# A hybrid HGRN2 and RWKV-7 layer: the transposes of values and keys, and the 64-token level, moved into the runs of HGRN's level products

## The chip, the core and the metric

The program runs on one core of a Trainium2 chip. The metric is the device time of one execution in microseconds. The core's engines are TensorE (PE in the profile; its weight loads are shown as PEld), VectorE (DVE), ScalarE (ACT), GpSimd (POOL) and SyncE (SP), which here only issues DMAs. They work side by side and wait for each other by semaphores.

## The reference, cut to what matters

The layer takes 2048 tokens of 1024 channels. After a norm and one input projection, half of the channels go through HGRN2, half through RWKV-7; one output projection and a feed-forward part with a convolution follow. HGRN2 is, for each of its 4 heads of 128 channels and in chunks of tokens:

```
f = lb + (1 - lb) * sigmoid(f_raw);  q = silu(q_raw) * 128**-0.5;  k = 1 - f;  v = i_raw;  logf = log(f)

def step(S, inp):                 # one chunk
    qb, kb, vb, gb = inp
    b = jnp.cumsum(gb, axis=2)
    dec = exp(b_t - b_s) for s <= t, else 0
    A = jnp.einsum('bhtk,bhsk,bhtsk->bhts', qb, kb, dec)
    o = jnp.einsum('bhts,bhsv->bhtv', A, vb) + jnp.einsum('bhtk,bhkv->bhtv', qb * jnp.exp(b), S)
    S = jnp.exp(b_last)[..., None] * S + jnp.einsum('bhsk,bhsv->bhkv', kb * jnp.exp(b_last - b), vb)
    return S, o

o = o * rsqrt(mean(o * o) + eps) * norm_w * silu(g_raw)
```

RWKV-7 is a second recurrence, with a matrix inverse of 32 by 32 and 64 by 64 in each chunk; the change does not touch it.

## The kernel before

The first phase (`phase1`) holds the input projection, both recurrences and three quarters of the output projection; it fills about the first half of the span. The second phase holds the rest of the output projection and the feed-forward part; the change doesn't touch it. Three generators run side by side in the first phase: `dense` (projections), `rw_stream` (RWKV, 8 pieces of 512 tokens and 4 heads each) and `hg_stream` (HGRN, 16 units: 4 blocks of 512 tokens by 4 heads). The loop at the end of `phase1` takes in each round one step of RWKV, one step of HGRN (each up to the generator's next `yield`) and then dense work for a credit of TICK = 2000 ns, at 648 ns for each step of three matmuls:

```python
        while any(alive.values()):
            for key, g in (("r", rw_), ("h", hg_)):
                if alive[key]:
                    ...
                        next(g)
            ...
            fill(TICK)
```

So the program text of the loop is nine dense products, a step of RWKV, a step of HGRN, nine dense products and so on. A scheduler then sets each engine's order from this text. A dense product (`mm3`, L270 to L272) is three matmuls of 128 by 128 by 512 that together have the precision of float32; L270, L271 and L272 stand for its three parts. PSUM has two banks of kind "hg" for HGRN, two of kind "pj" for the projection and two double banks of kind "rw".

A unit of HGRN (`hg_unit`) computes the products of a chunk by levels, so that no decay has to be divided by: level l pairs the two halves of each group of 2 x 2^l tokens. `scaled(l)` makes the operand X of a level on VectorE (for level 0 partly on ScalarE, the copies hX and Sf) from q, k and the running products of decays Pf and Sf; `level` are the products of 32 tokens by 32 or 16 columns for levels 0 to 4 (L990), `across` those of level 5 (L997), and the level of 64 tokens (level 6) has 64 by 64 products (L1046). The steps of a unit before the change are these:

- k = 1 - f (L947); values transposed into a bank (L952), copied to VT by ScalarE; then level operands 0, 1, 2, one step each
- a bank with the products of q and k within a token and levels 0 to 2 (L990, 64 products); VectorE takes them into A
- level operands 3, 4, 5, one step each; a second bank with levels 3, 4 (L990, 32 products) and 5 (L997, 8 products); ScalarE copies them and A into Af
- X of level 6, k * Sf and q * Pf on VectorE
- keys transposed into a third bank (L1044), the 64-token products into a fourth (L1046); ScalarE copies KT and the block of Af
- the state products KT by VT (L1055) and the chain of states SH on VectorE (L1057); the output products (L1064 by Af, L1065 by SH); squares, their mean by the matrix unit (L1083, L1084), Ln and Exp on ScalarE, the scaling, and a store of the result (L1078)

The result is built in a buffer that it shares with k (tag "hk"), so the next unit's k waits for the store. PSUM results are copied by `act` (L122). Ln and Exp, Sigmoid and Tanh, and Silu are in different function tables of ScalarE; `act` puts a table load (L118) where the program text goes over to another one. In RWKV's step before the state chain, matmuls L834 read the copies ZT, L847 read TTs; their results are copied as UV and M, which L867 and L881 read. L905 and L910 are the state chain's products, eight pairs one after the other, with VectorE between them.

Of the kernel before, what the change touches and what calls it, by code (L numbers as in the profile page):

```python
# [7 lines left out]
F32 = mybir.dt.float32  # L8
# [3 lines left out]
AF = mybir.ActivationFunctionType  # L12
# [6 lines left out]
P = 128  # L19
# [3 lines left out]
BLK = 512  # L23
# [44 lines left out]
def tile_layer(ctx, tc, consts, x, norm1_w, w_in, hg_lb_logits, hg_norm_w, rw_shift_mu, rw_w0, rw_w2,  # L68
# [4 lines left out]
    V, S, TE = nc.vector, nc.scalar, nc.tensor  # L73
# [200 lines left out]
    def phase1(c1):  # L274
# [22 lines left out]
        def bank(kind):  # L297
            return ps.tile([P, 512], F32, tag=kind, name=kind, bufs=2)
# [645 lines left out]
        def hg_unit(nb, j):  # L944
# [3 lines left out]

            VT = rp.tile([P, 4, P], F32, tag="VT", name="VT")
            tp = bank("hg")  # L950
            for b in range(4):
                TE.transpose(tp[:, b * P:(b + 1) * P], v[:, b * P:(b + 1) * P], ident)  # L952
            act(VT, tp.rearrange("p (b t) -> p b t", t=P), AF.Copy)
            yield
# [4 lines left out]

            def scaled(l):  # L960

                m = 1 << l
                X = rp.tile([P, BLK], F32, tag="hX", name="hX", bufs=3)
# [71 lines left out]
            yield  # L1035
            X = scaled(6)
            V.tensor_mul(k, k, Sf)
            V.tensor_mul(q, q, Pf)
            yield
            KT = rp.tile([P, 4, P], F32, tag="Sf", name="KT")  # L1040
            tp = bank("hg")
            lp = bank("hg")
            for b in range(4):
                TE.transpose(tp[:, b * P:(b + 1) * P], k[:, b * P:(b + 1) * P], ident)  # L1044
            for b in range(4):
                TE.matmul(lp[0:64, b * 64:b * 64 + 64], X[:, b * P:b * P + 64], X[:, b * P + 64:b * P + 128],  # L1046
                          start=True, stop=True, tile_position=(0, 0))
            act(KT, tp.rearrange("p (b t) -> p b t", t=P), AF.Copy)
            act(Af[0:64, :, 64:128], lp[0:64, 0:256].rearrange("p (b t) -> p b t", t=64), AF.Copy)
# [575 lines left out]
```

## Time and profile before

| | us |
|---|---|
| median of 3 runs | 2649.24 (2648.57 to 2652.3) |
| the profiled execution | 2645.42 |
| its span | 2643.6 |
| granted clock of TensorE, mean | 0.994 |
| PE busy | 2547.0 |
| VectorE busy | 1963.7 |
| ScalarE busy | 1372.7 |
| GpSimd busy | 382.1 |

The span is the time from the first to the last instruction of the profiled execution; the device time has 1.82 us around it. Lines of a timeline have the start, the length, the engine, the line of the kernel, the operation, output <- inputs, tile and shape. Lengths of matmuls overlap, since the next one starts while the one before drains.

### The profile page before, as it was taken

To read this page: it belongs to the slowest core of one execution; us is meant where nothing else is said; L and a number is where in the kernel's file an instruction comes from. 1 tells how busy PE (TensorE), PEld (TensorE's weight loads), DVE (VectorE), ACT (ScalarE), POOL (GpSimd) and SP (SyncE) were. 2 spreads that over 40 slices of the span, in tenths; PEclk is the share of its full clock that TensorE was granted. 3 is DMA by queue.
4 is the path that set the end of the run, shared out by engine and by line. 5 is a ranking of instruction groups with operands and counts; after the bars stand their busy time and mean duration, and the time that the engine had idled before them with its cause. 6 is when DMAs were issued, how large, how long until landed. Compare 5 with 4: busy or idle time off the path is not lost.

```text
span 2643.6 us, 51054 instructions
## 1 busy us (share of the span) xinstructions
PE 2547.0 (96%) x19467; PEld 2046.8 (77%) x19467; DVE 1963.7 (74%) x3744; ACT 1372.7 (52%) x2258; POOL 382.1 (14%) x686
## 2 busy tenths in 40 slices
PE   7999999999999999899899999999999999999998
PEld 5877777777777767777678888887888887888887
DVE  4868677676576765777678789988988887766556
ACT  5555444555545555344466654556554544545444
POOL 6433222212222122232100000000000000000000
PEclk9999999999999999999999999999999999999999
DMA  8846463555655565845583467747763553998655
GB/s 304 239 147 195 152 168 116 143 159 205 190 173 138 174 212 179 261 151 150 181 287 124 136 221 257 240 154 232 245 203 129 171 171 128 334 321 283 200 191 187
DMA packets 380298, 518.98 MB, mean 196 GB/s; under 512 B 114463, under 2 KB 211093, under 8 KB 380053
## 3 DMA queue, kind: packets, MB, share of 16 engines
q1 hardware_dynamic: 325521, 337.38, 40.1%
q0 software_dynamic: 54464, 178.32, 20.9%
q8 instruction: 153, 2.51, 0.4%
q14 instruction: 92, 0.75, 0.1%
q10 hardware_dynamic: 68, 0.02, 0.0%
HBM read 372.99 MB, written 134.22 MB: 192 GB/s over the span
## 4 chain that ended last, share of the span: by engine, by line
PE 70%; DVE 11%; ACT 8%; DMA 7%; issue 3%; POOL 0%; SPq 0%; DVEq 0%; ACTq 0%; POOLq 0%
PE pj L270 7%; PE pj L271 7%; PE pj L272 6%; PE ua L270 5%; PE ua L272 5%; PE ua L271 5%; PE da L271 3%; PE da L272 3%; PE da L270 3%; PE ud L271 2%; PE ud L270 2%; PE ud L272 2%; PE db L272 2%; PE db L271 2%; PE db L270 2%
## 5 line engine op out<-in xcount | busy, mean ns | idle before, releaser
L270 PE MATMUL pj<-hh,wh 128*128 128x512 f32 x960 | 391.6, 408 | 6.1 <-ACT rkv L122 4.0
L271 PE MATMUL pj<-hl,wh 128*128 128x512 f32 x960 | 377.4, 393 | 0.0
L272 PE MATMUL pj<-hh,wl 128*128 128x512 f32 x960 | 377.4, 393 | 0.0
L270 PE MATMUL ua<-Bh,uwh 128*128 128x512 f32 x704 | 276.4, 393 | 3.5 <-ACT m L122 2.2
L272 PE MATMUL ua<-Bh,uwl 128*128 128x512 f32 x704 | 274.3, 390 | 0.0
L271 PE MATMUL ua<-Bl,uwh 128*128 128x512 f32 x704 | 274.1, 389 | 0.0
L270 PEld LDWEIGHTS pj<-hh,wh 128*128 128x128 f32 x960 | 180.9, 189 | 54.5 <-issue 7.0
L272 PEld LDWEIGHTS pj<-hh,wl 128*128 128x128 f32 x960 | 180.8, 188 | 39.4 <-DMA wl<-Win171l 0.3
L271 PEld LDWEIGHTS pj<-hl,wh 128*128 128x128 f32 x960 | 181.0, 189 | 35.0 <-DVE hl L488 0.5
L254 ACT CAST uwh<-uraw 128x512 fp32r<-128x512 f32 x220 | 134.3, 617 | 135.0 <-PE ua L271 55.7
L255 DVE TENSOR_TENSOR dal<-draw,dah 128x512 fp32r<-128x512 f32 x138 | 95.2, 690 | 108.3 <-ACT dah L254 105.7
L255 DVE TENSOR_TENSOR uwl<-uraw,uwh 128x512 fp32r<-128x512 f32 x220 | 147.1, 684 | 34.3 <-ACT uwh L254 34.3
L254 ACT CAST dah<-draw 128x512 fp32r<-128x512 f32 x138 | 85.8, 621 | 160.0 <-PE da L271 75.5
L270 PEld LDWEIGHTS ua<-Bh,uwh 128*128 128x128 f32 x704 | 132.2, 188 | 33.9 <-ACT m L122 5.6
L272 PEld LDWEIGHTS ua<-Bh,uwl 128*128 128x128 f32 x704 | 132.2, 188 | 28.1 <-DVE uwl L255 0.4
L271 PEld LDWEIGHTS ua<-Bl,uwh 128*128 128x128 f32 x704 | 132.3, 188 | 26.7
L270 PE MATMUL ud<-Bh,uwh 128*128 128x512 f32 x352 | 138.0, 392 | 0.0
L1495 POOL DMA_DIRECT2D gd<-y x2 | 1.1, 542 | 943.1 <-DVE y L1493 943.1
L272 PE MATMUL ud<-Bh,uwl 128*128 128x512 f32 x352 | 137.1, 390 | 0.0
L271 PE MATMUL ud<-Bl,uwh 128*128 128x512 f32 x352 | 137.0, 389 | 0.0
L271 PE MATMUL da<-dbl,dah 128*128 128x512 f32 x332 | 129.4, 390 | 0.2 <-DVE dbl L255 0.2
L272 PE MATMUL da<-dbh,dal 128*128 128x512 f32 x332 | 129.2, 389 | 0.0
(582 smaller groups left out, 6203.0 us busy)
## 6 DMA issues: line engine op xcount, KB each, us to landing
uraw<-in_w_up_dram SPq DMA_DIRECT2D x176, 256.0 KB, 3.2
woraw<-in_w_out_dram POOLq DMA_DIRECT2D x96, 256.0 KB, 3.6
br<-gd SPq DMA_DIRECT2D x88, 256.0 KB, 4.3
draw<-Sg SPq DMA_DIRECT2D x88, 256.0 KB, 3.0
draw<-Tw SPq DMA_DIRECT2D x88, 256.0 KB, 3.9
gd<-y SPq DMA_DIRECT2D x86, 256.0 KB, 3.0
Sg<-br SPq DMA_DIRECT2D x72, 256.0 KB, 2.2
xt<-x1d SPq DMA_DIRECT2D x32, 512.0 KB, 6.5
```

Of the source, the lines that this page charges most:

```text
L254: S.copy(hi, src)
L255: V.tensor_sub(lo, src, hi.bitcast(F32))
L270: TE.matmul(acc, lh, rh, start=first, stop=False, skip_group_check=skip)
L271: TE.matmul(acc, lh, rl, start=False, stop=False, skip_group_check=skip)
L272: TE.matmul(acc, ll, rh, start=False, stop=last, skip_group_check=skip)
L1495: (dma if end is None else nc.gpsimd.dma_start)(gd_[2 * h + b][fb * P:(fb + 1) * P, :], ys[0][:, b * BLK:(b + 1) * BLK])
```

## The change

Nothing that is computed changes. Three things are moved.

- The transposes of the values leave the start of a unit and stand behind the products of levels 0 to 2, in the same step. A new helper `turned` holds the transposes and the copy, for values and keys alike (L957 in the changed kernel, where L990 has become L992, L997 is L999 and L1046 is L1036).
- Level 6 and the products k * Sf and q * Pf are made before the second bank is filled; the 64-token products go into the second bank's columns 256 to 512, behind levels 3 to 5, and the transposes of the keys follow in the same step. A unit so takes 7 banks of PSUM, not 8, and 13 steps, not 15.
- X of level 6 gets the buffer of SH, since the three buffers of hX are taken by levels 3 to 5.

```diff
-            VT = rp.tile([P, 4, P], F32, tag="VT", name="VT")
-            tp = bank("hg")
-            for b in range(4):
-                TE.transpose(tp[:, b * P:(b + 1) * P], v[:, b * P:(b + 1) * P], ident)
-            act(VT, tp.rearrange("p (b t) -> p b t", t=P), AF.Copy)
-            yield
...
+            def turned(tag, name, src):
+                t_ = rp.tile([P, 4, P], F32, tag=tag, name=name)
+                tp = bank("hg")
+                for b in range(4):
+                    TE.transpose(tp[:, b * P:(b + 1) * P], src[:, b * P:(b + 1) * P], ident)
+                act(t_, tp.rearrange("p (b t) -> p b t", t=P), AF.Copy)
+                return t_
+
             def scaled(l):
...
-                X = rp.tile([P, BLK], F32, tag="hX", name="hX", bufs=3)
+                X = (rp.tile([P, BLK], F32, tag="SH", name="hX6") if l == 6 else
+                     rp.tile([P, BLK], F32, tag="hX", name="hX", bufs=3))
...
             for l in range(3):
                 level(l1, l * 64, Xs[l], Xs[l], l)
+            VT = turned("VT", "VT", v)
             V.tensor_mul(A, ...)
...
             for l in range(3, 6):
                 Xs.append(scaled(l))
                 yield
+            X = scaled(6)
+            V.tensor_mul(k, k, Sf)
+            V.tensor_mul(q, q, Pf)
+            yield
             l1 = bank("hg")
             for l in range(3, 5):
                 level(l1, (l - 3) * 64, Xs[l - 3], Xs[l - 3], l)
             across(l1, 128, Xs[2])
+            for b in range(4):
+                TE.matmul(l1[0:64, 256 + b * 64:320 + b * 64], X[:, b * P:b * P + 64], X[:, b * P + 64:b * P + 128],
+                          start=True, stop=True, tile_position=(0, 0))
+            KT = turned("Sf", "KT", k)
...
-            yield
-            X = scaled(6)
-            V.tensor_mul(k, k, Sf)
-            V.tensor_mul(q, q, Pf)
-            yield
-            KT = rp.tile([P, 4, P], F32, tag="Sf", name="KT")
-            tp = bank("hg")
-            lp = bank("hg")
-            for b in range(4):
-                TE.transpose(...)
-            for b in range(4):
-                TE.matmul(lp[0:64, b * 64:b * 64 + 64], X[...], X[...], ...)
-            act(KT, tp.rearrange("p (b t) -> p b t", t=P), AF.Copy)
-            act(Af[0:64, :, 64:128], lp[0:64, 0:256].rearrange("p (b t) -> p b t", t=64), AF.Copy)
+            act(Af[0:64, :, 64:128], l1[0:64, 256:512].rearrange("p (b t) -> p b t", t=64), AF.Copy)
```

How the order on the engines changes is seen at three places. On PE, the first unit's second bank (L990 and L997) and its keys (L1044) and 64-token products (L1046), with dense products (L270 to L272, outputs pj) around them, before:

```order
374 L271 MATMUL pj<-hl,wh 128x512
375 L272 MATMUL pj<-hh,wl 128x512
376 L990 MATMUL hg<-hX 32x16 x32
377 L997 MATMUL hg<-hX 32x32 x8
378 L270 MATMUL pj<-hh,wh 128x512
...
395 L272 MATMUL pj<-hh,wl 128x512
396 L1044 MATMUL hg<-ident,hk 128x128 x4
397 L1046 MATMUL hg<-hX 64x64 x4
398 L270 MATMUL pj<-hh,wh 128x512
```

and the same place of the changed kernel:

```order
374 L271 MATMUL pj<-hl,wh 128x512
375 L272 MATMUL pj<-hh,wl 128x512
376 L992 MATMUL hg<-hX 32x16 x32
377 L999 MATMUL hg<-hX 32x32 x8
378 L1036 MATMUL hg<-hX_1399 64x64 x4
379 L957 MATMUL hg<-ident,hk 128x128 x4
380 L270 MATMUL pj<-hh,wh 128x512
```

The keys' transposes and the 64-token products have come forward by 18 dense products, into one run with the second bank, the narrow ones first. On PE, the values' transposes of the same unit stood alone before, between dense products:

```order
294 L271 MATMUL pj<-hl,wh 128x512
295 L272 MATMUL pj<-hh,wl 128x512
296 L952 MATMUL hg<-ident,hv 128x128 x4
297 L270 MATMUL pj<-hh,wh 128x512
298 L271 MATMUL pj<-hl,wh 128x512
```

and now stand behind the first bank's 64 products:

```order
323 L271 MATMUL pj<-hl,wh 128x512
324 L272 MATMUL pj<-hh,wl 128x512
325 L992 MATMUL hg<-hq,hk 32x32 x16
326 L992 MATMUL hg<-hX 32x16 x48
327 L957 MATMUL hg<-ident,hv 128x128 x4
328 L270 MATMUL pj<-hh,wh 128x512
```

Over the whole phase there are 247 runs of RWKV's and HGRN's products between dense products before and 213 after. On ScalarE, the first RWKV piece's copies TTs, UV and M, with HGRN's copy hX among them, before:

```order
104 L122 ACTIVATE TTs<-rw 32x8x32 x4
105 L122 ACTIVATE rkv_1763<-pj,omu 128x512
106 L254 CAST wh<-wraw 128x512
107 L122 ACTIVATE hX<-hk 128x256
108 L122 ACTIVATE UV<-rw 64x4x128 x4
109 L122 ACTIVATE M<-rw 128x8x64
```

and after:

```order
104 L122 ACTIVATE TTs<-rw 32x8x32 x2
105 L122 ACTIVATE hX<-hk 128x256
106 L122 ACTIVATE TTs<-rw 32x8x32 x2
107 L254 CAST wh<-wraw 128x512
108 L122 ACTIVATE rkv_1778<-pj,omu 128x512
109 L118 ACT_TABLE_LOAD
110 L122 ACTIVATE UV<-rw 64x4x128 x4
111 L122 ACTIVATE M<-rw 128x8x64
```

The copy hX has come ahead of two of the copies of TTs, and a table load stands ahead of UV: HGRN's steps meet other steps of RWKV than before. The table loads of the whole program are 53 before and 63 after. The loop has 383 rounds in both; HGRN ends in round 383 before and in round 379 after.

More of the change, by code (lines that the diff above doesn't have):

```diff
@@ L1034, in hg_unit @@
                 act(Af[c0:c0 + 32, :, c0:c0 + 32], A[c0:c0 + 32], AF.Copy)
-            yield
-            X = scaled(6)
-            V.tensor_mul(k, k, Sf)
-            V.tensor_mul(q, q, Pf)
-            yield
-            KT = rp.tile([P, 4, P], F32, tag="Sf", name="KT")
-            tp = bank("hg")
-            lp = bank("hg")
-            for b in range(4):
-                TE.transpose(tp[:, b * P:(b + 1) * P], k[:, b * P:(b + 1) * P], ident)
-            for b in range(4):
-                TE.matmul(lp[0:64, b * 64:b * 64 + 64], X[:, b * P:b * P + 64], X[:, b * P + 64:b * P + 128],
-                          start=True, stop=True, tile_position=(0, 0))
-            act(KT, tp.rearrange("p (b t) -> p b t", t=P), AF.Copy)
-            act(Af[0:64, :, 64:128], lp[0:64, 0:256].rearrange("p (b t) -> p b t", t=64), AF.Copy)
+            act(Af[0:64, :, 64:128], l1[0:64, 256:512].rearrange("p (b t) -> p b t", t=64), AF.Copy)
             yield
```

## The prediction

> **What bounds the kernel now.** I read the page first: its busy times, and the chain that ended last by engine.
>
> ```profile
> PE 2547.0 (96%) x19467; PEld 2046.8 (77%) x19467; DVE 1963.7 (74%) x3744; ACT 1372.7 (52%) x2258; POOL 382.1 (14%) x686
> PE 70%; DVE 11%; ACT 8%; DMA 7%; issue 3%; POOL 0%; SPq 0%; DVEq 0%; ACTq 0%; POOLq 0%
> ```
>
> PE is busy for 96% of the span and holds 70% of the chain, so a microsecond less of work on PE is worth nearly a microsecond, and a delay elsewhere costs only what PE then waits. The change lies in the first phase; so next the busy times of the two halves (columns: length, then busy time of PE, PEld, DVE, ACT, POOL, granted clock, DMA share, GB/s), and the waits of PE, a row for each waiting line and what it waited for.
>
> ```profile
> 0.00:1320.00 1320.00, 1239.12 (x13691) 970.71 (x13691) 911.21 (x2154) 667.56 (x1120) 368.10 (x660) 0.99 0.59 182
> 1320.00:2643.60 1323.60, 1307.92 (x5776) 1076.10 (x5776) 1052.51 (x1590) 705.14 (x1138) 14.04 (x26) 1.00 0.64 211
> PE rw L867 <- ACT M L122: 9.7, 6, 3.6
> PE rw L821 <- DVE TZ L808: 3.8, 4, 1.4
> PE hg L1055 <- ACT KT L122: 1.4, 2, 0.8
> PE rw L847 <- ACT TTs L122: 0.5, 1, 0.5
> PE rw L834 <- ACT ZT L122: 0.2, 1, 0.2
> ```
>
> In the first half PE is idle for 1320 - 1239.12 = 80.9 us, in the second for 15.7. All of HGRN's own waits are small: the state products of L1055, whose operand is the turned keys, wait 1.4 us in all. The largest wait inside the merged loop is RWKV's L867, 9.7 us in six times. So there are two things that this change can move: what PE spends in HGRN's short runs, and what it waits beside them. The pieces of a few runs, as the timeline of PE has them (start, length, then the line), price the first. A run here is HGRN's work between two dense products.
>
> ```profile
> 376.77 0.39 PE L272 MATMUL pj<-hh,wl 128*128 128x512 f32 x1
> 377.00 0.60 PE L952 MATMUL hg<-ident,hv 128*128 128x128 f32 x4
> 377.36 0.48 PE L270 MATMUL pj<-hh,wh 128*128 128x512 f32 x1
> 377.67 0.40 PE L271 MATMUL pj<-hl,wh 128*128 128x512 f32 x1
> ```
>
> ```profile
> 251.81 0.39 PE L272 MATMUL pj<-hh,wl 128*128 128x512 f32 x1
> 252.12 0.46 PE L990 MATMUL hg<-hq,hk 128*32 128x32 f32 x32
> 252.40 1.03 PE L990 MATMUL hg<-hX 128*32 128x16 f32 x96
> 253.36 0.50 PE L270 MATMUL pj<-hh,wh 128*128 128x512 f32 x1
> 253.70 0.39 PE L271 MATMUL pj<-hl,wh 128*128 128x512 f32 x1
> 253.93 0.40 PE L272 MATMUL pj<-hh,wl 128*128 128x512 f32 x1
> ```
>
> ```profile
> 398.44 0.39 PE L272 MATMUL pj<-hh,wl 128*128 128x512 f32 x1
> 398.76 0.72 PE L990 MATMUL hg<-hX 128*32 128x16 f32 x63
> 399.30 0.21 PE L997 MATMUL hg<-hX 128*32 128x32 f32 x1
> 399.31 0.18 PE L990 MATMUL hg<-hX 128*32 128x16 f32 x1
> 399.33 0.43 PE L997 MATMUL hg<-hX 128*32 128x32 f32 x15
> 399.69 0.50 PE L270 MATMUL pj<-hh,wh 128*128 128x512 f32 x1
> 400.02 0.39 PE L271 MATMUL pj<-hl,wh 128*128 128x512 f32 x1
> ```
>
> ```profile
> 403.67 0.39 PE L272 MATMUL pj<-hh,wl 128*128 128x512 f32 x1
> 403.90 0.60 PE L1044 MATMUL hg<-ident,hk 128*128 128x128 f32 x4
> 404.43 0.68 PE L1046 MATMUL hg<-hX 128*64 128x64 f32 x8
> 405.04 0.50 PE L270 MATMUL pj<-hh,wh 128*128 128x512 f32 x1
> 405.38 0.39 PE L271 MATMUL pj<-hl,wh 128*128 128x512 f32 x1
> ```
>
> Lengths overlap in the pipeline, so only starts are subtracted. Undisturbed dense products start 0.23 us apart (253.70 to 253.93). Going from dense to narrow tiles the step is longer, 0.31 (251.81 to 252.12) or 0.32 (398.44 to 398.76); into a transpose, which fills the array as the dense product does, it is 0.23 (403.67 to 403.90). The first dense product behind a run also steps long: 0.33 to 0.34 behind narrow tiles, 0.31 behind transposes. The cost of a run is the time from the start of the last product before it to that of the second product behind it, less two steps (0.46): values' transposes 377.67 - 376.77 - 0.46 = 0.44; first level run 1.43; second level run 1.12; keys' transposes with the 64-token products 1.25. Sum 4.24 us a unit, 16 units.
>
> **The two merged runs.** How transposes behave directly behind narrow tiles is seen where they follow a run of RWKV's (L905 and L910).
>
> ```profile
> 330.89 0.66 PE L1044 MATMUL hg<-ident,hk 128*128 128x128 f32 x4
> 331.48 0.68 PE L1046 MATMUL hg<-hX 128*64 128x64 f32 x8
> ```
>
> Here the transposes hold 0.59, against 404.43 - 403.90 = 0.53 behind a dense product: coming from narrow tiles costs 0.06. First run: step in 0.31, level products 253.36 - 252.12 = 1.24, transposes 377.36 - 377.00 = 0.36 and 0.06, the first dense step behind them 0.31, less 0.46: 1.82, in place of 1.43 + 0.44 = 1.87. It saves 0.05. Second run: 0.32 in, 399.69 - 398.76 = 0.93, the 64-token products 405.04 - 404.43 = 0.61, 0.36 + 0.06, 0.31, less 0.46: 2.13 in place of 1.12 + 1.25 = 2.37. It saves 0.24. So 0.29 a unit, 4.6 us over 16. That takes the step from the 32-wide tiles to the 64-wide ones at nothing, which no row shows; the nearest is transposes to 64-wide, 0.53 - 0.36 = 0.17, and with it the saving is 0.12 a unit, 1.9 us. From the other side: the instruction order has 247 such runs (RWKV's included) before and 213 after, 34 fewer, since some of the merged ones now also stand against a run of RWKV's; if each takes a whole way in and out of narrow tiles with it, (0.32 - 0.23) + (0.33 - 0.23) = 0.19, it is 6.5. I take 0.29 by 34 runs for 32, 4.6 x 34/32 = **-4.9**, ends -1.9 and -6.5.
>
> The Trainium skill's "TensorEngine Tiling (Array Packing)", Key Properties, says that changing the tiling mode, not just the tile, drains TensorE. The rows above agree (0.31 to 0.34 in place of 0.23), but the rule speaks against this change: the merged runs still hold full to 32-wide, 32 to 64 and back to full, so only one change of mode a unit is gone.
>
> **RWKV's L867.** The new order puts the first merged run between L847 and L867 in places where dense products stood. What costs most there now is in ScalarE's timeline (in brackets: idle before, and what ended it).
>
> ```profile
> 149.40 0.45 ACT L122 ACTIVATE hX<-hk 128x256 f32<-128x256 f32 x1 [3.65 <-DVE hk L947]
> 149.86 2.40 ACT L122 ACTIVATE UV<-rw 64x512 f32<-64x512 f32 x4
> ```
>
> ScalarE is queued behind HGRN's copy hX, which waits 3.65 us for k, whose buffer the unit before still has to store from; the copies of UV, ready by then, stand behind it, and PE at L867 waits 3.6 for what follows them. After the change that copy stands ahead of UV's, between copies of TTs. If its wait is covered there, 3.6 goes; at three of the other places the run of 1.24 and more stands for three products (0.69), which takes up to 0.55 each of their 9.7 - 3.6 = 6.1, 1.6 in all. If hX waits as long at its new place, TTs is late instead and only 1.6, or nothing, remains. Between 0 and 5.2 I take **-3.0**; the far end is all 9.7.
>
> **Ten more table loads.** In the order ScalarE loads its function tables 63 times, not 53: HGRN's Ln and Exp come two rounds earlier each unit and no longer meet RWKV's. The group of all loads, and one with its neighbours:
>
> ```profile
> L118 ACT ACT_TABLE_LOAD x53 | 68.0, 1283 | 1.7 <-PEq L1610 0.7
> 138.22 1.28 ACT L118 ACT_TABLE_LOAD   x1
> 139.51 0.69 ACT L122 ACTIVATE osq<-hg,eps 128x512 f32<-128x512 f32 x1
> ```
>
> Ten by 1.283 is 12.8 us of ScalarE, which is busy 667.56 of 1320: 51%. Five stand by the copies of ZT and TTs, for which PE now waits 0.2 and 0.5 us; five in rounds where RWKV's state chain runs on VectorE. Behind each stand mostly nine dense products, 9 x 0.23 = 2.07, longer than one load. Most are covered; I take one or two in full, **+2.0**, ends 0 and +12.8. The Trainium skill's "ScalarE: Activation LUTs", What ACT_TABLE_LOAD costs, gives 1.28 for the load and 1.38 more for a drain, 2.66 a switch; by that, my term would be an estimated 4.1 and the forecast 2 later. The trace agrees on the load and doesn't show the drain: the next instruction starts 0.01 behind it, and all 53 loads have 1.7 us of idle time before them.
>
> **The rest at nothing.** The values' transposes wait for nothing new (v is in SBUF long before); the keys' and the 64-token products now wait, in the first unit of a pair, for VectorE's k * Sf and X6, one step earlier than before, with nine or more products of PE's queue ahead; were that cover gone, the nearest row is 1.4 us in two waits (L1055). What is queued behind them is dense work, which the credit of the loop takes from the same list. L1055 still has nine products between it and the transposes in 14 of the units. One PSUM bank fewer is taken per unit, the first-level bank isn't held longer than a round, X6 in the buffer of SH is read before SH is written. Of DMAs only the stores of oT move, some rounds earlier, on SP and at last on POOL, where nothing waits for them. HGRN ends four rounds of 383 earlier and dense work fills PE there; the number of rounds is the same, as RWKV and dense work set it. All of this 0, ±2. The first half's clock of 0.99 means some 13 us of lost clock, in spells as here (two steps of 0.43):
>
> ```profile
> 1278.45 0.63 PE L271 MATMUL pj<-wl,hh 128*128 128x512 f32 x1
> 1278.88 0.63 PE L272 MATMUL pj<-wh,hl 128*128 128x512 f32 x1
> ```
>
> If other waits bring one spell more or fewer, I allow ±2.
>
> **Sum.** -4.9 - 3.0 + 2.0 = -5.9. The profiled execution took 2645.42 us (its span of 2643.60 and 1.82 around it), 3.82 below the median of 2649.24: the forecast is 2639.5 on its footing, 2643.3 on the median's. A measurement of this kernel can tell 0.2%, 5.3 us, from no change, so the forecast is just over that line.
>
> **Rivals.** *The switches stay (A).* Only one change of mode a unit goes, -1.9; PE, earlier at L867 and L821, waits again for VectorE and ScalarE, so of the 3.0 only 1.0 stays; loads +2.0. Together -0.9: 2648.3. For it: PE waits there already (9.7 and 3.8), and the step 32 to 64 isn't shown. Against: rows of 0.31 to 0.34 at every crossing, and 34 runs fewer. The tiling rule named above leads here.
>
> *ScalarE late (B), the slower side.* Ten loads, and hX with its 3.65, stand ahead of ZT's and TTs' copies, which PE reads at L834 and L847 within the round. In full 12.8 - 4.9 and no gain at L867: +7.9, 2657.1. It decides from 12.8 down to about 10.2 on the path (eight loads of ten): below that the merge brings it under +5.3. For it: ScalarE's order is fixed and DVE, the other engine in that chain, is busy 911 of 1320 (69%). Against: the present waits on ZT and TTs are 0.7 us together.
>
> *All of L867's waits go (C).* -4.9 - 9.7 + 2.0 = -12.6: 2636.6. It needs hX covered and every place filled; only four places are refilled.
>
> That the change doesn't do what it says is ruled out by the order of instructions: the merged runs stand there.
>
> **Chances.** Forecast 0.60, of itself 2639 to 2648 (-10 to -1.5), with 0.38 over 5.3 faster, 0.20 within and 0.02 slower by other things; A 0.17 (0.15 within, 0.02 slower); B 0.16, slower; C 0.07, faster. Faster 0.38 + 0.07 = 0.45, same 0.20 + 0.15 = 0.35, slower 0.02 + 0.02 + 0.16 = 0.20. Range 2635 to 2656: it takes in A, C and nearly all of B, and leaves out B in full and gains over 14.
>
> **What would show it.** Right: transposes behind L992 and L1036 without dense work between, crossing steps of 0.06 to 0.1 inside these runs, PE busy 4 to 6 us less in the first half; L867's row of waits at 5 to 8; 63 loads of 1.28 us with PE's waits for ZT and TTs under 3. Wrong: a start of the 64-token products 0.17 or more behind the 32-wide ones (A); waits of PE for ScalarE at L834, L847 or L867 above 15 us together (B); a new row of waits at L1036, L957 or L1055.

## The result and the profile after

The changed kernel takes 2663.09 us (median of 6 runs, 2659.04 to 2668.77), the kernel before on the same chip 2648.9 (6 runs): ratio 1.0051, 95% interval 1.0038 to 1.0065. It is slower by about 14 us, where 6 us faster was forecast, and outside the range on the other side.

The profiled execution took 2668.77 us, the slowest of the six; its span is 2667.0 and its clock 0.991, against 2643.6 and 0.994 before. A clock of 0.994 over 2643.6 us is 15.9 us lost, 0.991 over 2667.0 is 24.0. If every lost microsecond lengthened the span, 8 of the 23 us between these two executions would be clock; in the 24 runs of the kernel before beside the first experiments a line fitted to time and clock falls by 1.8 us for each 0.001, which makes it some 5. That is mostly their own luck: in those 24 runs the clock had a median of 0.992, in the six of the changed kernel 0.9915, a difference of 1 us. So a second trace of each follows below (c_before_again and c_after_again, on one chip).

The merged runs stand where the prediction has them. PE's timeline of the changed kernel, first bank and values' transposes, then second bank, 64-token products and keys' transposes (start, length):

```profile
731.35 0.39 PE L272 MATMUL pj<-hh,wl 128*128 128x512 f32 x1
731.67 0.46 PE L992 MATMUL hg<-hq,hk 128*32 128x32 f32 x32
731.94 1.03 PE L992 MATMUL hg<-hX 128*32 128x16 f32 x96
732.91 0.66 PE L957 MATMUL hg<-ident,hv 128*128 128x128 f32 x4
733.32 0.48 PE L270 MATMUL pj<-hh,wh 128*128 128x512 f32 x1
733.64 0.39 PE L271 MATMUL pj<-hl,wh 128*128 128x512 f32 x1
...
398.30 0.39 PE L272 MATMUL pj<-hh,wl 128*128 128x512 f32 x1
398.62 0.72 PE L992 MATMUL hg<-hX 128*32 128x16 f32 x63
...
399.19 0.43 PE L999 MATMUL hg<-hX 128*32 128x32 f32 x15
399.55 0.68 PE L1036 MATMUL hg<-hX 128*64 128x64 f32 x8
400.15 0.66 PE L957 MATMUL hg<-ident,hk 128*128 128x128 f32 x4
400.56 0.48 PE L270 MATMUL pj<-hh,wh 128*128 128x512 f32 x1
400.88 0.39 PE L271 MATMUL pj<-hl,wh 128*128 128x512 f32 x1
```

By the prediction's rule (last product before to second product behind, less 0.46) the first run costs 733.64 - 731.35 - 0.46 = 1.83 (1.82 worked out), the second 400.88 - 398.30 - 0.46 = 2.12 (2.13 worked out): 3.95 in place of 4.24, so 0.29 a unit is saved at these places. The first of them is the cheapest of its kind. In this trace the first run stands between dense products alone seven times and costs 1.83 to 2.07, in the median 1.94, against 1.44 + 0.44 = 1.88 for the medians of its two parts before; the second run costs 2.12 all five times that it stands alone. So the second merge saves its 0.25 and the first nothing that can be told: some 0.2 a unit, 3 us in place of 4.6. The step from the 32-wide to the 64-wide tiles, which no row of before showed, adds nothing to the second run's sum. Of the Trainium skill's rule that a change of tiling mode drains TensorE ("TensorEngine Tiling (Array Packing)", Key Properties) only the longer steps at either end are seen again.

The time is lost elsewhere. PE's waits in the kernel before, those rows that the prediction had not shown, and in the changed kernel (L1080 and L1081 are the mean of squares, L1083 and L1084 before; the columns are total, times and longest):

```profile
PE hg L1084 <- DVE part L248: 4.4, 7, 1.8
PE hg L1083 <- ACT part L247: 1.1, 2, 1.0
PE hg L990 <- issue: 0.4, 1, 0.4
```

```profile
PE hg L1081 <- DVE part L248: 7.4, 6, 1.6
PE hg L992 <- issue: 6.8, 5, 2.7
PE rw L867 <- ACT M L122: 6.0, 5, 2.2
PE hg L1080 <- ACT part L247: 4.5, 5, 1.7
PE rw L834 <- ACT ZT L122: 3.0, 4, 1.6
PE rw L847 <- ACT TTs L122: 2.4, 5, 0.7
```

Four things changed. L992, the first bank's products, waits 6.8 us in five places for something that the profile doesn't name ("issue"); before, 0.4. The mean of squares waits 11.9 for its two parts; before, 5.5. The copies ZT and TTs are waited for 5.4; before, 0.7. L867 waits 6.0, not 9.7. Together +6.4 +6.4 +4.7 -3.7 = +13.8. These rows are picked: PE's idle time in all rose less (9.6, below), so the other rows together fell by some 4. The waits for "issue" at all lines rose from 4.3 to 9.8.

By stretches: the first phase ends with its last dense product. The stretches up to there, PE's busy time second:

```profile
0.00:1312.93 1312.93, 1232.80 (x13666) 966.17 (x13667) 907.35 (x2148) 665.10 (x1116) 366.28 (x657) 0.99 0.59 181
```

```profile
0.00:1331.09 1331.09, 1241.39 (x13666) 971.06 (x13667) 912.77 (x2149) 681.58 (x1129) 366.61 (x658) 0.98 0.59 179
```

The phase is 18.2 us longer: PE is idle 89.7 us, not 80.1 (+9.6), and busy +8.6. How much of the busy time is clock can't be told closely. The kernel before in its second trace lost 13.2 us more to the clock (0.989 over 2645.0 us) and was only 6.4 busier:

```profile
0.00:1315.33 1315.33, 1239.23 (x13666) 973.02 (x13667) 907.51 (x2148) 664.57 (x1116) 364.96 (x657) 0.98 0.59 181
```

So busy time set right by the clock is uncertain by some 7 us, and these traces don't tell whether other work came to PE and hides what the merges save. The second phase, which the change doesn't touch, is 5.2 longer in this execution; 3.3 of that is idle time of PE.

### The profile page after: what moved, and what is told of

It reads as the page before. It is cut to its first block, busy times and chain, and to the rows that moved or that the text cites. A ratio compares the mean times of both kernels' runs of the same rounds, so it can differ in the third digit from the quotient of the medians.

```text
span 2667.0 us, 51044 instructions
## 1 busy us (share of the span) xinstructions
PE 2557.6 (96%) x19467; PEld 2052.8 (77%) x19467; DVE 1968.1 (74%) x3744; ACT 1387.5 (52%) x2268; POOL 381.7 (14%) x686
## 3 DMA queue, kind: packets, MB, share of 16 engines
q8 instruction: 153, 2.51, 0.4%
## 4 chain that ended last, share of the span: by engine, by line
PE 38%; DVE 11%; DMA 9%; issue 3%; ACT 3%; SPq 0%; DVEq 0%; ACTq 0%
PE ua L270 4%; PE ua L272 4%; PE ua L271 4%; PE da L271 2%; PE da L272 2%; PE da L270 2%; PE db L270 2%; PE db L272 2%; PE db L271 2%; PE ud L272 2%; PE ud L271 2%; PE ud L270 2%; DVE uwl L255 2%; DVE y L1484 1%; DMA br<-gd 1%
## 5 line engine op out<-in xcount | busy, mean ns | idle before, releaser
L270 PE MATMUL pj<-hh,wh 128*128 128x512 f32 x960 | 390.7, 407 | 4.7 <-ACT rkv L122 2.7
L272 PE MATMUL pj<-hh,wl 128*128 128x512 f32 x960 | 376.4, 392 | 0.0
L270 PE MATMUL ua<-Bh,uwh 128*128 128x512 f32 x704 | 277.1, 394 | 5.4 <-ACT uwh L254 3.0
L272 PE MATMUL ua<-Bh,uwl 128*128 128x512 f32 x704 | 275.3, 391 | 0.0
L270 PEld LDWEIGHTS pj<-hh,wh 128*128 128x128 f32 x960 | 181.3, 189 | 53.5 <-issue 10.0
L272 PEld LDWEIGHTS pj<-hh,wl 128*128 128x128 f32 x960 | 180.8, 188 | 38.9
L270 PEld LDWEIGHTS ua<-Bh,uwh 128*128 128x128 f32 x704 | 132.7, 188 | 35.9 <-ACT m L122 5.8
L272 PEld LDWEIGHTS ua<-Bh,uwl 128*128 128x128 f32 x704 | 132.6, 188 | 28.2 <-DVE uwl L255 0.4
L270 PE MATMUL ud<-Bh,uwh 128*128 128x512 f32 x352 | 138.1, 392 | 0.0
L272 PE MATMUL ud<-Bh,uwl 128*128 128x512 f32 x352 | 137.2, 390 | 0.0
L272 PE MATMUL da<-dbh,dal 128*128 128x512 f32 x332 | 129.3, 390 | 0.0
```

The costliest lines, as they stand in the source:

```text
L270: TE.matmul(acc, lh, rh, start=first, stop=False, skip_group_check=skip)
L272: TE.matmul(acc, ll, rh, start=False, stop=last, skip_group_check=skip)
```

## The experiments

Ratios are of timed runs against the kernel before on the same chip, with their 95% interval; us are medians. Three theories: *rounds* (with 13 steps in place of 15, HGRN's steps meet other steps of RWKV-7's), *merges* (the long runs themselves), *loads* (ten more table loads).

**e1_15_steps, both merges, the rounds of before.** Two empty steps added to the changed kernel:

```diff
             V.tensor_scalar(k, f, -1.0, 1.0, ALU.mult, ALU.add)
+            yield
...
             act(Af[0:64, :, 64:128], l1[0:64, 256:512]..., AF.Copy)
             yield
+            yield
```

> The changed kernel with two empty steps a unit: one behind k = 1 - f, one behind the step of the second bank. The level products stand in the merged runs, but the first bank, the state products, the output products and Ln and Exp fall in the same rounds of the loop as in the kernel before (15 steps a unit, 53 table loads in the order). Theory 1 (the rounds: with 13 steps HGRN meets other steps of RWKV-7, whose work on VectorE and ScalarE then stands ahead of its own): the waits go, the merged runs' saving of 0.29 by 16 = 4.6 us stays: 2644, ratio 0.998, L992 without waits. Theory 2 (the merged runs themselves are what costs, since they hold PE longer at a time or wait for more): still about 2663, ratio 1.005. Theory 3 (ten table loads on ScalarE): they are gone, so 2644 too; e5 tells it from theory 1.

Measured: 2657.89 against 2645.95, 1.0040 (1.0024 to 1.0057). The rounds theory fails as stated: with the rounds of before it should have been 2644.

**e2_before_13_steps, no merge, the rounds of after.** Two yields of the kernel before taken out:

```diff
             act(VT, tp.rearrange("p (b t) -> p b t", t=P), AF.Copy)
-            yield
...
                 act(Af[c0:c0 + 32, :, c0:c0 + 32], A[c0:c0 + 32], AF.Copy)
-            yield
             X = scaled(6)
```

> The kernel before with two of its yields taken out: values' transposes and level operand 0 in one step, second bank and level 6 in one step. No run on PE is merged; a unit has 13 steps, and its banks fall in the rounds in which the changed kernel has them; 63 table loads in the order. Theory 1 (the rounds): as slow as the changed kernel and slower by what its merged runs save, 14 + 4.6: 2668, ratio 1.007. Theory 2 (merged runs): 2649, ratio 1.000. Theory 3 (table loads): ten by 1.28 = 12.8 at most, 2662, ratio 1.005.

Measured: 2662.44, 1.0063 (1.0044 to 1.0082): +16.5 us with no run merged. Its waits (L989 is the first bank, L1081 and L1082 the mean):

```profile
PE hg L989 <- issue: 6.8, 4, 3.3
PE hg L1081 <- ACT part L247: 4.3, 4, 1.8
PE hg L1082 <- DVE part L248: 2.6, 3, 1.8
```

and its first phase:

```profile
0.00:1332.32 1332.32, 1249.14 (x13666) 973.13 (x13667) 914.11 (x2149) 681.06 (x1129) 368.06 (x658) 0.98 0.58 179
```

The 13 steps alone bring a loss as large as the changed kernel's, and the same new wait of 6.8 us at the first bank. (The second bank's level products stand one round earlier than in the changed kernel; that a round more or less for them costs anything couldn't be told at 15 steps, see e6.) Otherwise the loss lies elsewhere than in the changed kernel: PE's idle time in the first phase is 83.2, 3.1 over the first trace of before and 7.1 over the second, and the mean waits 6.9, not 11.9. The rest is busy time, 9.9 more than in the second trace of before, which had about the same clock (0.989, here 0.990). Where PE is busy longer the traces don't show.

**e5_more_loads.** The kernel before with `tab["now"] = None` behind each unit's Exp.

> The kernel before, unmoved, where each unit's Exp makes ScalarE load a table anew at the next function that needs one: 61 loads in the order in place of 53. Theory 3 (table loads): each load 1.28 us on the path, 8 by 1.28 = 10.3: 2659, ratio 1.004. Theories 1 and 2: the loads lie beside PE's dense work: 2649 to 2651, ratio 1.000 to 1.001.

Measured: 2649.38, 1.0016 (1.0001 to 1.0030): 4 us for eight loads, 8 at most; by that, ten cost some 5, 10 at most. The loads alone are not the loss of 14, and e7 and e8 below, with 63 loads, lose 3 and 6.

**e3_values_only** and **e4_second_only.** Each merge by itself, in 15 steps. e3 moves the four transposes and the copy VT behind the first bank and leaves the empty step; e4 is e1 with those lines at the start again.

> The kernel before, where only the values' transposes are moved behind the first bank's level products; the empty step stays, so all rounds are as before (15 steps, 53 loads). Theory 1: 0.05 by 16 = 0.8 us less, 2648, ratio 0.9997. Theory 2: if the longer first run delays RWKV-7's steps behind it, a part of the 14 us shows here: 2652 or more, ratio 1.001 or more. Theory 3: nothing, 2649.

> As e1 (15 steps, all else in the rounds of before), but only the second bank, the 64-token products and the keys' transposes are one run; the values' transposes stay at the start. If e1's 12 us come from the second merge or what it moves: 2657, ratio 1.004. If from both merges together: 2650 to 2653. If the runs were merged for free: 16 by 0.24 = 3.8 less than before, ratio 0.9985.

Measured: e3 2648.13 against 2645.95, 1.0010 (0.9996 to 1.0024); e4 2646.72 against 2647.86, 0.9996 (0.9987 to 1.0004). Neither alone costs or gains anything that can be told. e1, which is both, costs 12: they don't add.

**c_before_again, c_after_again.** Both kernels, unchanged, one run each.

> The kernel before, unchanged, profiled on the same chip as the other kernels of this call: a second trace of it, to tell what of a difference between two profiled executions is theirs alone (spells of half clock above all). All theories: 2640 to 2652, PE's idle time in the first phase within 5 us of the first profile's 69.0, L1055 with the small waits of before.

> The changed kernel, unchanged, profiled on the same chip: a second trace. Theory 1 (rounds): the waits of L992 (6.8 us in the first trace), of L1080 and L1081 (11.9) and of L834 and L847 (5.4) come again within a third, since the order of instructions sets them; if they don't, they were that execution's alone. 2655 to 2669.

2646.81 and 2670.57. The changed kernel's waits come again to a tenth or two of a microsecond in their sums where HGRN waits:

```profile
PE hg L1081 <- DVE part L248: 7.2, 6, 1.7
PE hg L992 <- issue: 6.9, 5, 3.2
PE hg L1080 <- ACT part L247: 4.5, 5, 1.8
PE rw L867 <- ACT M L122: 4.1, 4, 2.2
PE rw L847 <- ACT TTs L122: 2.2, 4, 0.7
PE rw L834 <- ACT ZT L122: 1.9, 4, 0.6
```

So the order of instructions sets these sums, not the execution (the longest wait of L992 is 3.2 here, 2.7 in the first trace). Those of RWKV's copies, 4.1 here and 5.4 in the first trace, come again less closely. Their first phases end at 1315.33 and 1335.28 us, 20.0 apart, with PE's idle time 76.1 and 88.1. In both pairs of traces, then, 10 to 12 of the 23 to 24 us between the spans are idle time of PE in the first phase.

**e6_late_bank.** 15 steps, no merge; level 6 one step earlier, the second bank one step later:

```diff
+            X = scaled(6)
+            V.tensor_mul(k, k, Sf)
+            V.tensor_mul(q, q, Pf)
+            yield
             l1 = bank("hg")
...
-            yield
-            X = scaled(6)
-            V.tensor_mul(k, k, Sf)
-            V.tensor_mul(q, q, Pf)
             yield
```

> The kernel before with 15 steps and no run merged, where level 6 and the products k * Sf and q * Pf come one step earlier and the second bank one step later (X of level 6 in the buffer of SH), and the keys' transposes and 64-token products stay where they were. It does what the second merge has to do before it can merge. If the later second bank (its copies to Af and the predicated copies on VectorE one round later, level 6 a round earlier) is what made e1 slow: 2656, ratio 1.004. If the merged run itself is: 2646, ratio 1.000.

Measured: 2647.31, 1.0008 (0.9996 to 1.0019). What the second merge has to move first costs nothing that can be told at 15 steps.

**What L992 waits for.** One of its five waits in the changed kernel's first trace, on PE:

```profile
934.28 0.31 PE L992 MATMUL hg<-hq,hk 128*32 128x32 f32 x10
934.72 0.70 PE L881 MATMUL rw<-M 64*64 64x64 f32 x32
935.21 0.68 PE L881 MATMUL rw<-KBT,M 64*64 64x64 f32 x32
935.81 0.36 PE L992 MATMUL hg<-hq,hk 128*32 128x32 f32 x19
...
936.01 0.79 PE L992 MATMUL hg<-hX 128*32 128x16 f32 x68
939.51 0.43 PE L992 MATMUL hg<-hX 128*32 128x16 f32 x27 [2.70 <-issue]
```

The wait falls in the middle of one bank's products, between two that need nothing new. From 934.28 to the wait, in some 2.5 us, 165 small matmuls stand, with a weight load each (two rows with 4 of them are left out). The page's list of DMA queues counts what instructions are fetched, and the same list for the window from 936.8 to 939.5 us follows:

```profile
q8 instruction: 153, 2.51, 0.4%
```

```profile
q8 instruction: 1, 0.02, 2.3%
```

153 pieces are 2.51 MB, 16 KB each; PE has 2 x 19467 = 38934 matmuls and weight loads, 254 to a piece. That the queue is PE's is seen in p2 below, which leaves out 1024 matmuls and as many weight loads; there it moves 8 pieces fewer, 256 instructions each:

```profile
q8 instruction: 145, 2.38, 0.4%
```

In the window from 934 to 936.8 us the list has no piece; the next one moves within the wait, and PE goes on behind it. So the reading is that PE, among small products, uses up its instructions faster than the next piece comes. Between dense products, each 0.23 us, 127 matmuls and so a piece last an estimated 30 us. The times of the pieces in the traces bear it out. In the changed kernel's first trace all five waits of L992 end 1.4 to 1.6 us behind the end of a piece, though only 108 pieces move in the 1331 us of the phase. Over all twenty traces 90 of the 127 waits for "issue" of 0.15 us or more in the first phase end 1.2 to 1.7 us behind one, 39 of the 42 that last 1 us or more among them; the other 37 are at L867 (up to 0.3 us) and at L270 (up to 1.2).

The next kernels test whether the length of the runs brings these waits. In the order of instructions (one entry is two matmuls in the trace, for a transpose one) the longest run of small products has 104 entries before and 132, 131 and 127 in the changed kernel, where the first bank stands with L867 and L881 or, in the run of 131, with L834 and L847. But the wait shown is in none of these. Its run has 100 entries, like those of two more of the five, and these three hold 5.1 of the 6.8 us; the 3.3 us wait of e2 is in a run of 87. So the length of a run alone doesn't tell where PE waits.

**e7_14_front** and **e8_14_back.** The changed kernel with one of e1's two empty steps each: 14 steps.

> The changed kernel with one empty step behind k = 1 - f (14 steps a unit, 63 loads, both merges). The traces so far show that the waits of L992 are waits for instructions: PE's instructions come in pieces of 16 KB, and where the first bank stands in one run with RWKV-7's L867 and L881 (127 to 132 products, in the order) the next piece comes late. Here the longest run is 108. Supply theory: L992's waits 6.8 us fall under 2. Rounds theory as a whole: the time is neither that of 13 nor of 15 steps but set by which steps meet: with 5 us less of L992's waits 2651 to 2659, ratio 1.002 to 1.005.

> The changed kernel with one empty step behind the second bank instead (14 steps, 63 loads, both merges). Here the order has three runs of 132 products, more than in the changed kernel (132, 131, 127). Supply theory: L992's waits stay at 5 us or more. The mean's waits (L1080, L1081) are open: they come from which of RWKV-7's steps ScalarE and VectorE do in that round. 2655 to 2668, ratio 1.003 to 1.008.

e7: 2650.14 against 2647.07, 1.0011 (0.9995 to 1.0028), the first bank's wait 1.5. e8: 2652.58, 1.0021 (1.0009 to 1.0032), the wait 2.5, where 5 or more was expected. One step more takes back more than half of the loss, at either place, and both times are a little under the ranges expected. The first bank's wait is the longer one in e8, but half of what three runs of 132 were to cost, and only 0.5 us of it is in one of those three runs. In all, both kernels wait 6.7 us for "issue".

**p2_fewer_products, p2_again, p3_before_fewer.** Levels 1 and 2 are left out of the first bank (A takes level 0's columns in their place; the numbers computed are others), in the changed kernel (p2) and in the kernel before (p3):

```diff
             for l in range(3):
-                level(l1, l * 64, Xs[l], Xs[l], l)
+                if l == 0:
+                    level(l1, l * 64, Xs[l], Xs[l], l)
...
-                take(l, l1, l * 64)
+                take(l, l1, 0)
```

> The changed kernel, all steps as they are, but the first bank leaves out the products of levels 1 and 2 (32 of its 64; A takes level 0's columns in their place, so the numbers computed are others). Supply theory: the runs with L867 and L881 have 100 products, not 132, and L992's waits of 6.8 us go under 2. If L992 waited for an operand of VectorE or ScalarE, the waits stay, on whatever comes last. In both, 16 x 0.4 = 6 us of work less.

> The changed kernel with the same omission, now timed: supply theory: it loses the omitted work, 10, and a part of the changed kernel's waits (L992 6.8, and what follows from them), 2643 to 2649, ratio 0.999 to 1.001. If the long runs cost nothing, only the work goes: 2653, ratio 1.002.

> The kernel before, with levels 1 and 2 left out of the first bank (A takes level 0's columns in their place), as p2 does in the changed kernel: what the omission is worth where no run is long. Work: 64 of 128 matmuls of the first bank, about 0.6 us by 16 = 10: 2637, ratio 0.996. If p2's fall of some 20 us is the omitted work and nothing else, it is 2627 here too.

p3: 2636.19 against 2647.59, 0.9956 (0.9940 to 0.9972): the omission is worth 11.4 in the kernel before. p2: 2639.23, 0.9975 (0.9960 to 0.9990); a single run earlier had 2646.47. Against the changed kernel, 1.0051 of 2647.59 = 2661.1, it is 21.9 less. The omission takes 10.5 more from the changed kernel than from the one before, by the intervals of the three ratios give or take 7; with it they are 3 us apart, not 14. p2's waits:

```profile
PE rw L834 <- ACT ZT L122: 9.3, 8, 3.6
PE hg L1081 <- ACT part L247: 3.6, 2, 1.9
PE hg L1082 <- DVE part L248: 1.6, 3, 0.9
```

No wait of the first bank is left, and the mean's (L1081 and L1082 here) fell from 11.9 to 5.2; the wait for ZT rose to 9.3, and L881's for AR from 3.5 to 8.3. The 10.5 is more than the supply theory's own 6.8, but the traces don't show it as idle time: in the first phase PE is idle 85.6 in p2, 4.1 under the changed kernel, and 75.4 in p3, 4.7 under the kernel before.

**e9_mean_later.** 13 steps; an empty step ahead of the mean, levels 5 and 6 in one step.

```diff
                 Xs.append(scaled(l))
-                yield
+                if l != 5:
+                    yield
...
             split_to(hi, lo, sq)
             yield
+            yield
```

> The changed kernel with an empty step between the output products and the mean of squares, and levels 5 and 6 in one step, so that a unit still has 13 steps: second bank, state and output products come one round earlier, first bank and mean stay. If L1080 and L1081 wait (11.9 us in all) because one round is too short for the squares and their two parts on ScalarE and VectorE, two rounds cover it: these waits under 3, time 2654, ratio 1.003. If the time lies in the 13 steps otherwise, 2660 or more stays. L992 as in the changed kernel, 5 or more.

Measured: 2662.88 against 2647.07, 1.0053 (1.0034 to 1.0071). The mean's waits went to 1.9 us, as expected, and the time stayed: the wait for ZT is 5.9 here and the first bank's 3.4. Taking the mean's wait away brought nothing that can be told: the seven runs of e9 had a median clock of 0.989, those of the kernel before 0.992, and at 1.8 us for each 0.001 that is 5 us, which could hide a gain.

**e10_split_bank.** 13 steps, no work left out; the first bank cut in two:

```diff
             level(l1, 192, k, q)
-            for l in range(3):
+            level(l1, 0, Xs[0], Xs[0], 0)
+            yield
+            for l in range(1, 3):
                 level(l1, l * 64, Xs[l], Xs[l], l)
...
                 Xs.append(scaled(l))
-                yield
+                if l != 3:
+                    yield
```

> The changed kernel with the first bank cut in two: the products of q and k and level 0 in one step, levels 1 and 2 with the values' transposes in the next, and levels 3 and 4 made in one step, so that a unit still has 13 steps; no work is left out. The longest runs have 115 and 100 products, not 132. Supply theory: L992's waits go under 2; the cut costs one more way in and out of narrow tiles, 0.19 by 16 = 3. With the 13 steps' other waits left, 2655 to 2661, ratio 1.003 to 1.005. Rounds theory with no part for the supply of instructions: 2663 to 2667.

Measured: 2665.7 against 2647.59, 1.0069 (1.0049 to 1.0089). The first bank's wait fell to 2.2, but the time didn't:

```profile
PE hg L1084 <- DVE part L248: 5.1, 5, 1.3
PE hg L1083 <- ACT part L247: 4.5, 5, 1.7
PE hg L992 <- issue: 2.2, 4, 1.1
```

The profiled execution, 2657.82, is the fastest of the six. PE's busy time in its first phase is 1239.9 us at a clock that loses 8 us less than in the changed kernel's first trace (0.994 against 0.991): set right by the clock, 6.5 more than there, which is within the uncertainty of 7 found above. That the cut cost what the shorter wait gave is therefore not shown. The mean's waits, 9.6, are nearly the changed kernel's.

**e12_before_14** and **e11_second_14.** e12 is e2 with the first yield put back; e11 is e4 without its empty step behind the second bank. Both have 14 steps and e7's rounds (the second bank of e12 stands one round earlier).

> The kernel before with one yield less: second bank and level 6 in one step, 14 steps, no run merged, 63 loads. The banks fall in the rounds of e7. If the merged runs are worth their 4.6 us of PE's work at 14 steps too, this is e7 (3 us over before) and 4.6 more: 2655, ratio 1.003. If the merges are worth nothing in the end, 2650, ratio 1.001.

> e12 with the second merge alone (14 steps; the values' transposes at the start in their own step, as before). Rounds as in e7 and e12. With 0.24 by 16 = 3.8 less work than e12: 2651, ratio 1.0015; it has one run of 162 products in the order, so by the supply of instructions one wait of 2 to 3 us more, 2653.

e12: 2652.85 against 2645.7, 1.0033 (1.0021 to 1.0044), +7 as expected, with 8.2 us of waits of its first bank for instructions. e11: 2658.81, 1.0050 (1.0033 to 1.0067), where 2651 to 2653 was expected. Its waits:

```profile
PE hg L998 <- issue: 6.2, 3, 2.8
PE rw L847 <- ACT TTs L122: 4.4, 7, 1.5
PE rw L881 <- issue: 4.2, 2, 3.2
```

With a third at L895, 2.7, and small ones it waits 16.5 us for instructions in all, the most of any kernel here; its longest run has 162 entries, but only 2.3 of the 16.5 us are in that run.

**e1_again.** The kernel of e1 once more.

> The kernel of e1 (15 steps, both merges) once more, for a second trace and on another day's footing: whether its 12 us over the kernel before come again (2658), and which of its waits do: in the first trace L1064 4.5, L881 behind the supply of instructions 3.3, wl 5.5. A wait that comes again within a third belongs to the order; one that doesn't was that execution's.

2656.78 against 2645.7, 1.0035 (1.0021 to 1.0049): the loss comes again, and with it these waits (first trace: 5.5, 4.5, 3.3).

```profile
PE pj L271 <- DVE wl L255: 5.0, 7, 2.3
PE hg L1064 <- DVE SH L1056: 4.5, 3, 1.7
PE rw L881 <- issue: 3.0, 1, 3.0
```

**All of it beside each other.** "Instructions" is the sum of PE's waits for "issue" in the traces.

| kernel | steps | merges | ratio | instructions, us |
|---|---|---|---|---|
| before (two traces) | 15 | none | 1 | 4.3, 1.9 |
| e5 (eight more loads) | 15 | none | 1.0016 | 1.8 |
| e6 | 15 | none | 1.0008 | 4.4 |
| e3 | 15 | first | 1.0010 | 0.2 |
| e4 | 15 | second | 0.9996 | 2.2 |
| e1 (two traces) | 15 | both | 1.0040, 1.0035 | 7.8, 6.8 |
| e12 | 14 | none | 1.0033 | 9.1 |
| e7 | 14 | both | 1.0011 | 6.7 |
| e8 | 14 | both | 1.0021 | 6.7 |
| e11 | 14 | second | 1.0050 | 16.5 |
| e2 | 13 | none | 1.0063 | 11.5 |
| changed (two traces) | 13 | both | 1.0051 | 9.8, 8.4 |
| e9 | 13 | both | 1.0053 | 6.1 |
| e10 | 13 | both, bank cut | 1.0069 | 3.1 |

The column takes in the waits at L867 and L270 that no piece goes with, 1.7 us at most. Where it is under 4.5 us the kernel is as fast as before or nearly so, and where it is over 8 it is slower. e10 doesn't fit, with 3.1 and the largest ratio, and between the two the column doesn't tell them apart: e7 and e8 lose 3 and 6 us at 6.7, e9 loses 14 at 6.1. No version that computes the same is faster than the kernel before; e4 is level with it.

## Why the prediction was wrong

- **The merged runs, -4.9.** Half right: 0.29 a unit at the places priced, with nothing for the step from 32-wide to 64-wide tiles, but some 0.2, or 3 us, over all the places where the runs stand alone, since the first merge saves nothing there. At 13 and 14 steps the kernels with both merges are faster than those with none by 1.0063 against 1.0051 and 1.0033 against 1.0011, 3 and 6 us; the intervals overlap in both pairs. At 15 steps the two merges together lose 11, and each alone nothing: the gain is there in the runs that stand alone and does not carry over. PE's busy time in the first phase, of which 4 to 6 us less was to be a sign of being right, is 8.6 us more in the first pair of traces and 8.0 in the second, clock included.
- **L867, -3.0.** Right in size, and by the reason given in part: 9.7 went to 6.0 (second traces 7.7 and 4.1). At the place that was shown, L867's 3.6 went to 0.9, 2.7 of the 3.7; in the second pair hX had waited only 2.1 us and L867 went from 2.0 to 0.9 there, 1.2 of 3.6. ScalarE's copy hX in its new place waits for nothing:

```profile
142.16 0.78 ACT L122 ACTIVATE TTs<-rw 32x256 f32<-32x256 f32 x2
142.84 0.42 ACT L122 ACTIVATE hX<-hk 128x256 f32<-128x256 f32 x1
143.27 0.76 ACT L122 ACTIVATE TTs<-rw 32x256 f32<-32x256 f32 x2
```

- **Ten table loads, +2.0.** Right in kind: 63 loads of the same length, and eight more of them cost 4 us (0 to 8) in e5.

```profile
L118 ACT ACT_TABLE_LOAD x63 | 80.8, 1283 | 1.8 <-PEq L1607 0.7
```

  The idle time before all 63 is 1.8 us, so the drain that the Trainium skill adds to each load ("ScalarE: Activation LUTs", What ACT_TABLE_LOAD costs) isn't in this trace either. ZT's and TTs' waits rose by 4.7, to 5.4, where under 3 was to be a sign of being right; part of that may be loads. Rival B, at +7.9, had the sign and about half of the loss, but nearly all of it from the loads, which by e5 cost some 5 us.
- **"The rest at nothing", 0, ±2.** This is the step that failed: "HGRN ends four rounds of 383 earlier and dense work fills PE there; the number of rounds is the same". It priced the two steps fewer per unit at the tail of the phase, and not where each unit's steps now meet RWKV's. e2, which has that and no merge, loses 16.5 us in place of 0, ±2. Two parts of it the trace of before could have suggested: PE's waits for instructions, 4.3 us at six lines on "issue"; and the mean's waits of 5.5, in a step with one round for ScalarE and VectorE. The prediction had read the same list as "All of HGRN's own waits are small"; the mean's rows L1083 and L1084 are HGRN's and were left out, and they became 11.9. A third part, the longer busy time of PE in e2, no row of before shows. None of the three stands under "Wrong" in the prediction, which for new waits looked at L1036, L957 and L1055: the first two have none, and L1055 (L1052 now) waits 2.0, not 1.4.
- **The clock, ±2.** Right for medians (0.992 and 0.9915). Single executions differ by more: the kernel before went from 2639.56 to 2657.8 in 24 runs, and from 2639.56 to 2651.88 in those at the same clock of 0.992.

What is shown: the 13 steps alone, without a merge, cost as much as the change (16.5 against 14); the new waits recur; PE's idle time in the first phase is 10 to 12 of the 23 to 24 us between the traces of the two kernels; most waits for "issue" end 1.2 to 1.7 us behind the arrival of a piece of instructions; the loads are 10 us at most, and the clock is small in the medians. What isn't shown is that the merges cost nothing. Each alone costs nothing at 15 steps, and at 13 and 14 both together cost nothing more, but at 15 both together lose 11 to 12. So the loss doesn't divide into a part for the steps and a part for the merges. Nor does it divide by waits: those for instructions go with the loss in most kernels, but e10 has few of them and the largest ratio, e9 loses as much as the changed kernel with fewer, and the omission in p2 removed more than they are. Of e1 the waits that recur are 4.5 for SH, 3.0 to 3.3 for instructions at L881 and 5.0 to 5.5 for wl (2.7 before), but e4 has the 4.5 for SH too and loses nothing. The 5.2 and 3.8 us by which the second phase is longer in the changed kernel's traces are idle time of PE for 3.3 and 0.7; the rest is busy time, and why they come stays open. In e2's, 2660.5 - 1332.3 = 1328.2, it is 2.5 shorter than before.

## What to carry to other kernels

Where a loop hands out one step of each of several streams per round, a yield is not only a cut: taking two out of one stream moves every later step of it against the other streams, and that has to be priced by itself, best by a run that removes the yields and nothing else. A saving worked out from starts of instructions on the busiest engine can be right to a hundredth of a microsecond at one place, smaller over all places, and lost to the meetings that it rearranges. PE's instructions come in pieces: where a profile has waits without a named cause among small matrix products, compare their ends with the times of the pieces, and don't judge by the length of the runs alone. And before a difference between two traces is set right by the clock, two traces of the same kernel show how far that correction holds.

## What the hardware showed that was not expected

PE waited up to 3.3 us at the first bank's products for no cause that the profile names, five times in the changed kernel and four in e2. In the one shown, 165 small matmuls had been issued within some 2.5 us; a piece of 16 KB holds about 254 of PE's instructions, none moved in the 2.8 us before the wait and one within it, and PE went on 1.4 us behind its end. No kernel changed the supply by itself, so that it is the cause is argued, from this and from the 90 of 127 such waits that end 1.2 to 1.7 us behind a piece. And one kernel on one chip spread over 18 us in 24 runs, more than the change itself moved; its spells of half clock (clock 0.986 to 0.993) go with the time only in part.
